# Differential attention in a two-layer decoder kernel: the first place with two steps of projection taken one unit earlier, and the norms of the second queries queued behind that place's weighing

## The chip, the cores and the metric

The kernel runs on one core of one Trainium2 chip. The metric is the device time of one execution in microseconds (us). The kernel before the change took 1323.74 us, the median of three runs (1322.02 to 1325.03).

## The reference, cut to what matters

The trunk has two layers over 512 tokens of width 1024. Layer 0 is a state-space mixer followed by a gated feed-forward block with a short causal convolution. Layer 1 is differential attention with 8 heads, followed by a second feed-forward block. The change lies in the attention of layer 1, whose core is this:

```python
q = (rms_norm(x, ln_g) @ q_w).reshape(b, s, ATT_HEADS, 2, ATT_HEAD_DIM)
q = rms_norm(q, q_norm_g)
...
logits = jnp.einsum('bqhcd,bkhcd->bhcqk', qblk, k).astype(jnp.float32) * scale
logits = logits + bias[None, :, None]
logits = jnp.where(dist >= 0, logits, -jnp.inf)
p = jax.nn.softmax(logits, axis=-1)
attn = p[:, :, 0] - lam * p[:, :, 1]
return jnp.einsum('bhqk,bkhd->bqhd', attn.astype(v.dtype), v)
...
o = rms_norm(o, subln_g) * (1.0 - lam_init)
return o.reshape(b, s, V_TOTAL) @ out_w
```

Each head has two softmax maps of 512 x 512, causal, which are subtracted with a learned weight. Keys and values come from the stream after layer 0, and they are computed once. Every query, and every head's output, is normed on its own.

## The kernel before, in words

Everything is float32. A large product is made of three TensorE matmuls over operands that are split into a high and a low part (`wh`, `wl` for a weight, `xgh`, `xgl` for the stream). Weights come in chunks: SyncE starts the load of a raw chunk (`wr_...`, three buffers), ScalarE writes its high half (`wh_...`, three buffers) and VectorE its low half (`wl_...`, three buffers).

The attention runs as one weave on TensorE, whose order is written out by hand. Two kinds of work are woven together.

**Units.** A head is cut into three units by rows of queries: part 0 holds the first two blocks of 128 queries, part 1 the third, part 2 the fourth. With 8 heads there are 24 units, counted by `t`; unit 10, for instance, is part 1 of head 3. A unit has four stages:

- `logits`: TensorE makes the logits of both maps (`lg`), VectorE adds the bias and finds the maximum (`mx`, line 1504), ScalarE takes the exponential (line 1512).
- `weigh`: VectorE subtracts the second map from the first (lines 1519 to 1525).
- `turn`: TensorE transposes the weighed map (`at`, line 1534), ScalarE copies it out of PSUM.
- `values`: TensorE multiplies by the values (`po`, line 1545), ScalarE scales the result into the head's output `ot` (line 1548).

When all three units of a head have their values, the head's output is normed: ScalarE squares it (`osq`, line 1555), VectorE sums it (`so`, line 1556), the reciprocal root is made in small steps on both engines (lines 494 to 499), and VectorE multiplies (`ot`, line 1558). Later `turned_out` transposes the normed output on TensorE (`oT`, line 1564); ScalarE and VectorE write its halves `oh` and `ol` (lines 1567 and 1568), which the output projection uses.

**Fill.** Between the stages of the units TensorE does steps of the projections that are still to come: the rest of the first half of the values, the second half of the queries (`q1`, heads 4 to 7), the second half of the values (`v1`), then the first part of the output projection. One `next(fill)` is one step: 12 matmuls of 512 columns, for two blocks of tokens (`ps_v1_0` and `ps_v1_1`, or `ps_v1_2` and `ps_v1_3`) and one chunk of weights (`wh_v1_0` is the chunk with rows 0 and 1 of the eight row blocks, `wh_v1_2` the next, and so on).

After the last step of `q1` its queries are normed (`head_norm`): VectorE multiplies four tiles `knq1_0` to `knq1_3` by the reciprocal root (line 1350). Their transposes (`ktq1_0` to `ktq1_3`, line 1357) are put in the list `late`; `proj` calls an entry of it when the step reaches the place that the entry names. Place (2, 0) is behind chunk 2, token block 0 of `v1`, and place (2, 1) behind token block 1. ScalarE copies the transposes to `qT1` (line 1358), which head 4 needs.

How many fill steps follow each unit is a list of numbers, `places`. At a place with one step and `t < 16`, the head output that is due (`out_of(t)`) is transposed ahead of the step. At a place with two steps it is transposed behind the first of them. A head's output is due five units after its last unit; head 1 is due at `t = 10`.

TensorE runs in the order of the program. On the other engines a scheduler picks the order when the program is built, and every engine then runs its own row of instructions in that fixed order. There are eight PSUM banks: four for the projections (`mm_bank`) and four for everything that is transposed or small (`aux_bank`), so that a new small tile waits until an earlier one has been read.

Of the kernel before, what the change touches and what calls it, by code (L numbers as in the profile page):

```python
# [13 lines left out]
ALU = mybir.AluOpType  # L14
# [4 lines left out]
P = 128  # L19
# [3 lines left out]
NT = T // P  # L23
# [18 lines left out]
def trunk_kernel(ctx: ExitStack, tc, x, ssm_ln_g, ssm_in_w, ssm_conv_w, ssm_conv_b, ssm_dt_bias,  # L42
# [4 lines left out]
    act, dve, pool, pe, sync = nc.scalar, nc.vector, nc.gpsimd, nc.tensor, nc.sync  # L47
# [14 lines left out]
    def aux_bank(name):  # L62
        return pp.tile([P, T], F32, tag="aux", name=name)
# [452 lines left out]
    def along_tokens(r, name):  # L516

        ps = aux_bank("al_" + name)
        for b in range(NT):
            pe.transpose(ps[:, b * P:(b + 1) * P], r[:, b:b + 1].to_broadcast([P, P]), ident)  # L520
        return ps
# [76 lines left out]
    with tc.tile_pool(name="ssm_y", bufs=1) as yp, tc.tile_pool(name="ssm", bufs=1) as sp:  # L598
# [29 lines left out]
        with tc.issue_after(b1_end.ins):  # L628
            for c in range(NT):
# [11 lines left out]
                          in1=dtb.unsqueeze(1).to_broadcast([P, NT, NH]), op=ALU.add)  # L641
# [7 lines left out]
        for n in (13, 11, 9, 7, 5, 3):  # L649
# [6 lines left out]
                                 in1=alog.unsqueeze(1).to_broadcast([P, NT, NH]),  # L656
# [228 lines left out]
        def normed(g, xs, rt):  # L885
            with tc.issue_after(state["last"]):
                r = along_tokens(rt, "g%d" % g)
            yh, yl = [], []
            for b in range(4):
                h = yp.tile([P, T], F32R, tag="yh", name="yh%d_%d" % (g, b), bufs=5)  # L890
                l = yp.tile([P, T], F32R, tag="yl", name="yl%d_%d" % (g, b), bufs=5)
                dve.scalar_tensor_tensor(out=xs[b], in0=xs[b], scalar=c2[:, 4 * g + b:4 * g + b + 1],
                                         in1=r, op0=ALU.mult, op1=ALU.mult)
                act.activation(h, xs[b], AF.Copy)
                dve.tensor_tensor(out=l, in0=xs[b], in1=h.bitcast(F32), op=ALU.subtract)
                yh.append(h)
                yl.append(l)
            return yh, yl
# [3 lines left out]
        for g in range(NG):  # L902
# [40 lines left out]
            else:  # L943
                op = out_proj(g - 1, *prev, None)
# [338 lines left out]
    with tc.tile_pool(name="att", bufs=1) as ap, ExitStack() as later:  # L1283
        rts = []
        late = []
# [59 lines left out]

        def head_norm(key, kn, ss, dst, gcol, where):
            rsqrt_act(ss, ap, key, [P, NT, 8], 64)
            for b in range(NT):
                v = kn[b].rearrange("p (a q) -> p a q", a=8)
                dve.tensor_tensor(out=v, in0=v, in1=ss[:, b, :].unsqueeze(2).to_broadcast([P, 8, 64]),  # L1350
                                  op=ALU.mult)

            def turned(bs):
                for b in bs:
                    ps = aux_bank("kt%s_%d" % (key, b))
                    for h in range(4):
                        pe.transpose(ps[:, h * P:(h + 1) * P], kn[b][:, h * P:(h + 1) * P], ident)
                    act.activation(dst[:, :, b * P:(b + 1) * P], ps.rearrange("p (h t) -> p h t", h=4),
                                   AF.Copy, scale=c2[:, gcol:gcol + 1])

            for at, bs in zip(where, ((0, 1), (2, 3))):
                late.append((at, lambda bs=bs: turned(bs)))
# [255 lines left out]
        with tc.manual_schedule(engines={mybir.EngineType.PE}):  # L1618
# [42 lines left out]
            def weigh_to(m):  # L1661
                nonlocal weighed
                while weighed < min(m, n):
                    us[weighed].weigh()
                    weighed += 1
# [4 lines left out]
                    values(valued)  # L1670
                    valued += 1

            for places in [(2, 2), 1, 1, 1, 1, 1, 1, 1, 1, 1, 2, 1, 1, 1, 1, 2, 1, 2, 1, 2, 1, 2, 2, 1, 1, 1]:
                if isinstance(places, tuple):
                    weigh_to(t)
                    turn_to(t - 1)
                    values_to(t - 2)
                    norm_heads()
                    turn_to(t)
                    next(fill)  # L1680
                    out_of(t + 1)
                    values_to(t)
                    norm_heads()
                    next(fill)
                    us[t].logits()
                    us[t + 1].logits()
                    weigh_to(t + 1)
                    next(fill)
                    weigh_to(t + 2)
                    next(fill)  # L1690
                    t += 2
                    continue
                turn_to(t - 1)
                if t == n - 5:
                    weigh_to(t)
                    with tc.issue_after(us[t - 1].weighed):
                        us[t].logits()
                elif t < n:
                    us[t].logits()
                weigh_to(t)  # L1700
                values_to(t - 2)
                for i in range(places):
                    if places == 1 and t < 16:
                        out_of(t)
                    next(fill)
                    if i == 0 and (places > 1 or t > n):
                        out_of(t)
                    if valued_heads and os:
                        with tc.issue_after(state["ol"]):
                            norm_heads()  # L1710
                    norm_heads()
                t += 1
# [40 lines left out]
```

## Time and profile before

| what | value |
|---|---|
| median of three runs | 1323.74 us |
| the profiled execution | 1323.59 us |
| its span in the trace | 1321.9 us |
| TensorE matmul busy | 1313.3 us, 99% of the span |
| VectorE busy | 1094.1 us, 83% |
| ScalarE busy | 722.5 us, 55% |
| GpSimd busy | 176.2 us, 13% |
| mean granted TensorE clock | 0.999 |

The profiled execution lies 0.15 us below the median of the runs, and 1.69 us of it lie outside the span. In the rows of the trace, PE is TensorE's matmul, PEld its load of weights, DVE is VectorE, ACT ScalarE, POOL GpSimd and SP SyncE. A row of the timeline gives the start in us from the span's start, the duration in us, engine, line, operation, what is written and what is read, how many instructions are merged, and in brackets the idle time ahead of it with the work that ended it. Matmuls overlap each other at their ends, so the step from one start to the next is what a matmul costs, not its duration.

### The profile page before, as it was taken

The numbers are of one execution on the slowest core, as the hardware profiler recorded it, in microseconds if no ns is written. First come the engines' busy times: TensorE is split into PE (matmuls) and PEld (weight loads), VectorE is DVE, ScalarE is ACT, GpSimd is POOL, SyncE is SP. The second block draws the span as 40 slices with busy tenths as digits, with TensorE's granted clock in tenths as the row PEclk, the third lists the DMA queues.
The fourth block names the chain that finished last, engine by engine and source line by source line (L and its number), as shares of the span: only waits on it lengthen the run. The fifth ranks groups of instructions, "written<-read, shape, count | busy, mean of one in ns | idle before, by whom it ended". The sixth has DMA issues, their size and how long they took to land. (4 is left out here: it accounts for less than half of the span.)

```text
span 1321.9 us, 18303 instructions
## 1 busy us (share of the span) xinstructions
PE 1313.3 (99%) x6771; PEld 1097.8 (83%) x6771; DVE 1094.1 (83%) x1834; ACT 722.5 (55%) x1176; POOL 176.2 (13%) x243
## 2 busy tenths in 40 slices
PE   9999999999999999999999999999999999999998
PEld 8878888888888988898889887767888878888887
DVE  7989888788878878886889877778778978887887
ACT  6696554743454545543556676767654534444452
POOL 4330200300121401110113210000020100010001
PEclk9999999999999999999999999999999999999999
DMA  7553533532235657674856854211225445453635
GB/s 209 161 154 87 146 108 103 145 92 79 80 96 149 118 149 205 167 155 128 225 143 143 208 129 125 64 57 56 65 80 159 97 119 178 106 99 112 191 64 128
DMA packets 202553, 167.85 MB, mean 127 GB/s; under 512 B 7580, under 2 KB 175904, under 8 KB 202464
## 3 DMA queue, kind: packets, MB, share of 16 engines
q1 hardware_dynamic: 176080, 124.93, 31.8%
q0 software_dynamic: 22928, 36.46, 14.8%
q10 hardware_dynamic: 3456, 5.30, 1.1%
q8 instruction: 53, 0.87, 0.3%
q14 instruction: 36, 0.29, 0.1%
HBM read 160.21 MB, written 6.44 MB: 126 GB/s over the span
## 5 line engine op out<-in xcount | busy, mean ns | idle before, releaser
L207 PE MATMUL ps_u<-xgh,wh_u 128*128 128x512 f32 x352 | 137.4, 390 | 0.0
L209 PE MATMUL ps_g<-xgh,wl_g 128*128 128x512 f32 x352 | 137.1, 389 | 0.0
L207 PE MATMUL ps_g<-xgh,wh_g 128*128 128x512 f32 x352 | 137.1, 389 | 0.0
L209 PE MATMUL ps_u<-xgh,wl_u 128*128 128x512 f32 x352 | 137.0, 389 | 0.0
L208 PE MATMUL ps_g<-xgl,wh_g 128*128 128x512 f32 x352 | 137.0, 389 | 0.0
L208 PE MATMUL ps_u<-xgl,wh_u 128*128 128x512 f32 x352 | 136.9, 389 | 0.0
L207 PE MATMUL ps_in<-xgh,wh_in 128*128 128x512 f32 x304 | 122.9, 404 | 0.0
L209 PE MATMUL ps_in<-xgh,wl_in 128*128 128x512 f32 x304 | 119.7, 394 | 0.0
L208 PE MATMUL ps_in<-xgl,wh_in 128*128 128x512 f32 x304 | 119.1, 392 | 0.0
L209 PEld LDWEIGHTS ps_g<-xgh,wl_g 128*128 128x128 f32 x352 | 66.1, 188 | 14.0 <-DVE wl_g L158 0.3
L208 PEld LDWEIGHTS ps_g<-xgl,wh_g 128*128 128x128 f32 x352 | 66.1, 188 | 13.7
L1228 PE MATMUL ps_s<-sl,wh_s 128*128 128x256 f32 x308 | 77.5, 283 | 0.0
L209 PEld LDWEIGHTS ps_u<-xgh,wl_u 128*128 128x128 f32 x352 | 66.1, 188 | 13.7
L1227 PE MATMUL ps_s<-sh,wh_s 128*128 128x256 f32 x308 | 77.5, 283 | 0.0
L208 PEld LDWEIGHTS ps_u<-xgl,wh_u 128*128 128x128 f32 x352 | 66.1, 188 | 13.6
L207 PEld LDWEIGHTS ps_g<-xgh,wh_g 128*128 128x128 f32 x352 | 66.1, 188 | 13.6
L207 PEld LDWEIGHTS ps_u<-xgh,wh_u 128*128 128x128 f32 x352 | 66.1, 188 | 13.5
L1118 ACT ACTIVATE sh<-vg 128x256 fp32r<-128x256 f32 (+1 forms) x44 | 23.0, 524 | 96.0 <-DVE vg L1266 96.0
L1047 POOL DMA_DIRECT2D wz<-in_ffn_down_w_dram x36 | 44.2, 1295 | 233.3 <-DVE wl_s L1075 156.1
L1262 ACT ACTIVATE vg<-vg 128x512 f32<-128x512 f32 x44 | 27.8, 633 | 78.7 <-DVE vg L1019 78.7
L1019 DVE SCALAR_TENSOR_TENSOR vg<-ug,cf,vg 128x511 f32<-128x511 f32 x88 | 65.8, 748 | 5.5 <-ACT vg L1017 4.1
L147 ACT ACTIVATE wh_u<-wr_u 128x1024 fp32r<-128x1024 f32 x44 | 46.6, 1059 | 42.5 <-PE ps_g L208 35.4
(430 smaller groups left out, 3527.1 us busy)
## 6 DMA issues: line engine op xcount, KB each, us to landing
wr_g<-in_ffn_up_w_dram SPq DMA_DIRECT2D x44, 512.0 KB, 3.9
wr_u<-in_ffn_up_w_dram SPq DMA_DIRECT2D x44, 512.0 KB, 4.0
wr_in<-in_ssm_in_w_dram SPq DMA_DIRECT2D x40, 512.0 KB, 3.9
wz<-in_ffn_down_w_dram POOLq DMA_DIRECT2D x27, 512.0 KB, 5.9
m<-cumd POOLq DMA_DIRECT2D x16, 512.0 KB, 5.0
wr_out<-in_ssm_out_w_dram SPq DMA_DIRECT2D x16, 512.0 KB, 3.5
wr_s<-in_ffn_down_w_dram SPq DMA_DIRECT2D x13, 512.0 KB, 3.8
xT<-in_ffn_down_w_dram SPq DMA_DIRECT2D x10, 512.0 KB, 7.0
```

Of the source, the lines that this page charges most:

```text
L147: return act.activation(self.wh[:, :self.n], self.raw[:, :self.n], AF.Copy)
L207: pe.matmul(ps, wh, xh, start=start, stop=False)
L208: pe.matmul(ps, wh, xl, start=False, stop=False)
L209: return pe.matmul(ps, wl, xh, start=False, stop=stop).ins
L1019: dve.scalar_tensor_tensor(out=v[:, s:], in0=u[:, :T - s], scalar=col(2 - s), in1=v[:, s:], op0=ALU.mult, op1=ALU.add)
L1047: pool.dma_start(view(t, nq), source(p0, c, nq, j, i), accum_op=ALU.add)
L1118: act.activation(sh[:, o], v, AF.Copy)
L1227: pe.matmul(v[:, b], wh[:, q, cols], h, start=q == 0, stop=False)
L1228: pe.matmul(v[:, b], wh[:, q, cols], w, start=False, stop=False)
L1262: act.activation(ga, ga, AF.Silu)
```

## The change

In `places`, the first single number 2 moves from unit 11 to unit 10. And the four multiplications that norm the second queries are no longer written where `head_norm` is called, but put in `late` with the place (0, 3): behind chunk 0, token block 3 of `v1`.

```diff
         def head_norm(key, kn, ss, dst, gcol, where):
             rsqrt_act(ss, ap, key, [P, NT, 8], 64)
-            for b in range(NT):
-                v = kn[b].rearrange("p (a q) -> p a q", a=8)
-                dve.tensor_tensor(out=v, in0=v, in1=ss[:, b, :].unsqueeze(2).to_broadcast([P, 8, 64]),
-                                  op=ALU.mult)
+            def normed():
+                for b in range(NT):
+                    v = kn[b].rearrange("p (a q) -> p a q", a=8)
+                    dve.tensor_tensor(out=v, in0=v, in1=ss[:, b, :].unsqueeze(2).to_broadcast([P, 8, 64]),
+                                      op=ALU.mult)
+
+            if key == "q1":
+                late.append(((0, 3), normed))
+            else:
+                normed()
...
-            for places in [(2, 2), 1, 1, 1, 1, 1, 1, 1, 1, 1, 2, 1, 1, 1, 1, 2, 1, 2, 1, 2, 1, 2, 2, 1, 1, 1]:
+            for places in [(2, 2), 1, 1, 1, 1, 1, 1, 1, 1, 2, 1, 1, 1, 1, 1, 2, 1, 2, 1, 2, 1, 2, 2, 1, 1, 1]:
```

The rows below give the order of instructions on an engine, cut to the places that the change moves. In the changed kernel all lines behind the edit stand six lower, so that L1570 there is L1564 before; L1350 becomes L1351. A number behind a tile's name counts buffers.

TensorE at units 10 and 11, before: `po2_1` are the values of part 1 of head 2, `oT1` the transposed output of head 1, `ps_v1_2` a fill step's first block, `at3_0`, `lg3_2` and `po2_2` the stages of unit 11's turn, `ktq1` the transposes of the second queries.

```order
L1545 MATMUL po2_1_8281<-vt2_6963,at2_1_8180 128x128
L1564 MATMUL oT1_8286<-ident_77,ot1_8028 128x128 x4
L1325 MATMUL ps_v1_2_8234<-wh_v1_0_7964,xgh_86 128x512
...
L1534 MATMUL at3_0_8308<-ident_77,lg3_0_0_8192 128x128 x3
L1498 MATMUL lg3_2_0_8317<-kT0_6957,qT0_6959 128x512
L1498 MATMUL lg3_2_1_8318<-kT0_6957,qT0_6959 128x512
L1545 MATMUL po2_2_8330<-vt0_6961,at2_2_8256 128x128
...
L1325 MATMUL ps_v1_0_8232<-wh_v1_2_8088,xgh_86 128x512
...
L1357 MATMUL ktq1_0_8350<-ident_77,knq1_0_8106 128x128 x4
L1357 MATMUL ktq1_1_8356<-ident_77,knq1_1_8111 128x128 x4
...
L1357 MATMUL ktq1_3_8374<-ident_77,knq1_3_8162 128x128 x4
```

The same place of TensorE with the change:

```order
L1551 MATMUL po2_1_8277<-vt2_6963,at2_1_8180 128x128
L1325 MATMUL ps_v1_2_8230<-wh_v1_0_7964,xgh_86 128x512
...
L1570 MATMUL oT1_8298<-ident_77,ot1_8028 128x128 x4
L1325 MATMUL ps_v1_0_8228<-wh_v1_2_8088,xgh_86 128x512
...
L1363 MATMUL ktq1_0_8321<-ident_77,knq1_0_8106 128x128 x4
L1363 MATMUL ktq1_1_8327<-ident_77,knq1_1_8111 128x128 x4
...
L1363 MATMUL ktq1_3_8345<-ident_77,knq1_3_8162 128x128 x4
L1540 MATMUL at3_0_8352<-ident_77,lg3_0_0_8192 128x128 x3
L1504 MATMUL lg3_2_0_8361<-kT0_6957,qT0_6959 128x512
L1504 MATMUL lg3_2_1_8362<-kT0_6957,qT0_6959 128x512
L1551 MATMUL po2_2_8374<-vt0_6961,at2_2_8252 128x128
```

The 12 matmuls of the step with `ps_v1_2` and `ps_v1_3` now stand ahead of `oT1`, and the next step, with the transposes of the queries, stands ahead of unit 11's `at3_0`, `lg3_2` and `po2_2`. The number of instructions on TensorE is the same.

VectorE from the normed output of head 1 to the low half of its transpose, before: `lg3_0_0` is the weighing of unit 9 in its two pieces, `knq1` the norms of the second queries, `ol1` the low half of `oT1`.

```order
L1558 TENSOR_TENSOR ot1_8028<-ot1_8028,so1_8168 128x512
...
L1525 SCALAR_TENSOR_TENSOR lg3_0_0_8192<-lg3_0_1_8193,sm3_0_8191,lg3_0_0_8192 128x128
L1350 TENSOR_TENSOR knq1_0_8106<-knq1_0_8106,ssq1_7751 128x512
...
L1350 TENSOR_TENSOR knq1_3_8162<-knq1_3_8162,ssq1_7751 128x512
L1525 SCALAR_TENSOR_TENSOR lg3_0_0_8192<-lg3_0_1_8193,sm3_0_8191,lg3_0_0_8192 128x256
L1568 SCALAR_TENSOR_TENSOR ol1_8292<-oT1_8286,c2_89,oh1_8291 128x512
```

The same place of VectorE with the change; `wl_v1_6` is the low half of a chunk of weights:

```order
L1564 TENSOR_TENSOR ot1_8028<-ot1_8028,so1_8168 128x512
...
L1531 SCALAR_TENSOR_TENSOR lg3_0_0_8192<-lg3_0_1_8193,sm3_0_8191,lg3_0_0_8192 128x128
L1531 SCALAR_TENSOR_TENSOR lg3_0_0_8192<-lg3_0_1_8193,sm3_0_8191,lg3_0_0_8192 128x256
L1351 TENSOR_TENSOR knq1_0_8106<-knq1_0_8106,ssq1_7751 128x512
...
L1351 TENSOR_TENSOR knq1_3_8162<-knq1_3_8162,ssq1_7751 128x512
L1574 SCALAR_TENSOR_TENSOR ol1_8304<-oT1_8298,c2_89,oh1_8303 128x512
L173 SCALAR_TENSOR_TENSOR wl_v1_6_8310<-wr_v1_6_8307,c2_89,wh_v1_6_8309 128x512 x2
```

The second piece of unit 9's weighing goes from behind the four norms to ahead of them. Everything on VectorE up to the normed output of head 1 keeps its order.

ScalarE behind the last exponential of unit 10, before: `oh1` is the high half of `oT1`, `wh_v1_6` the high half of a chunk, in two pieces, `at3_0` the copy of unit 9's transposed map.

```order
L1512 ACTIVATE lg3_1_1_8266,sm3_1_8264<-lg3_1_1_8266,mx3_1_8263 128x384
L1567 ACTIVATE oh1_8291<-oT1_8286,c2_89 128x512
L172 ACTIVATE wh_v1_6_8338<-wr_v1_6_8336,c2_89 128x512
L1535 ACTIVATE at3_0_8307<-at3_0_8308 128x384
L172 ACTIVATE wh_v1_6_8338<-wr_v1_6_8336,c2_89 128x512
```

The same place of ScalarE with the change; `qT1` are the copies of the transposed queries:

```order
L1518 ACTIVATE lg3_1_1_8262,sm3_1_8260<-lg3_1_1_8262,mx3_1_8259 128x384
L172 ACTIVATE wh_v1_6_8309<-wr_v1_6_8307,c2_89 128x512
L1573 ACTIVATE oh1_8303<-oT1_8298,c2_89 128x512
L172 ACTIVATE wh_v1_6_8309<-wr_v1_6_8307,c2_89 128x512
L1364 ACTIVATE qT1_6960<-ktq1_0_8321,c2_89 128x4x128
...
L1364 ACTIVATE qT1_6960<-ktq1_3_8345,c2_89 128x4x128
L1541 ACTIVATE at3_0_8351<-at3_0_8352 128x384
```

The first piece of `wh_v1_6` now stands ahead of `oh1`, and the four copies of the transposed queries stand ahead of the copy of unit 9's map. SyncE's and GpSimd's rows, all transfers among them, keep their order.

## The prediction

> **What bounds the kernel now.** I read the page's busy times first, then the waits of TensorE, then the timeline round the place of the change.
>
> ```profile
> span 1321.9 us, 18303 instructions
> PE 1313.3 (99%) x6771; PEld 1097.8 (83%) x6771; DVE 1094.1 (83%) x1834; ACT 722.5 (55%) x1176; POOL 176.2 (13%) x243
> PE oT L1564 <- DVE ot L1558: 2.8, 1, 2.8
> ```
>
> TensorE is busy for 1313.3 us of a span of 1321.9 us, so time can only go where TensorE does less, or idles less, or runs at a better clock. The change leaves its matmuls as many as they were. Of the waits that the view names, the largest is a single one of 2.8 us: the transpose of a head's normed output (`oT`) for VectorE's multiplication. The timeline shows it at unit 10, the very place that the change reorders:
>
> ```profile
> 861.91 0.94 PE L1545 MATMUL po<-vt,at 128*128 128x128 f32 x6
> 865.61 1.03 PE L1564 MATMUL oT<-ident,ot 128*128 128x128 f32 x4 [2.76 <-DVE ot L1558]
> 866.30 0.78 PE L1325 MATMUL ps_v<-wh_v,xgh 128*128 128x512 f32 x1
> ...
> 868.58 0.63 PE L1327 MATMUL ps_v<-wh_v,xgl 128*128 128x512 f32 x1
> 869.00 0.47 PE L1325 MATMUL ps_v<-wh_v,xgh 128*128 128x512 f32 x1
> ```
>
> The wait costs more than itself. The windows view (length; busy time and count of PE, PEld, DVE, ACT, POOL; granted clock; transfers) has the whole piece from `po2_1` to the next projection step, the same kinds and counts of work at units 13 and 14, where nothing waits, and then the idle stretch and the one behind it:
>
> ```profile
> 861.91:872.86 10.95, 8.19 (x40) 6.19 (x38) 8.43 (x30) 6.68 (x22) 0.00 (x0) 0.84 0.17 49
> 886.41:892.79 6.38, 6.38 (x39) 4.88 (x38) 4.66 (x13) 3.72 (x9) 0.00 (x0) 1.00 0.01 3
> 862.85:865.61 2.76, 0.00 (x0) 0.00 (x1) 2.15 (x13) 2.65 (x11) 0.00 (x0) 1.00 0.65 190
> 865.61:869.00 3.39, 3.39 (x10) 2.82 (x11) 3.39 (x10) 1.38 (x5) 0.00 (x0) 0.52 0.01 2
> ```
>
> 10.95 us against 6.38: this piece loses 4.57 us. 2.76 are idle; and for 3.39 us behind it the granted clock is 0.52, so that matmuls stand 0.42 us apart (868.58 to 869.00) where they stand 0.23 apart elsewhere. That second part is worth about 1.57: the four transposes and six matmuls took 3.39, and by the rows below they take 0.35 + 1.47.
>
> [...]
>
> **The change, part by part.** It adds and removes no instruction. It moves 12 matmuls (`ps_v1_2`, `ps_v1_3`) ahead of `oT1`, and the next step of 12, with the 16 transposes of the second queries, ahead of unit 11's `at3_0`, `lg3_2` and `po2_2`. These rows carry the steps between starts:
>
> ```profile
> 857.01 0.94 PE L1545 MATMUL po<-vt,at 128*128 128x128 f32 x6
> 857.70 0.47 PE L1325 MATMUL ps_v<-wh_v,xgh 128*128 128x512 f32 x1
> 860.54 0.60 PE L1534 MATMUL at<-ident,lg 128*128 128x128 f32 x4
> ...
> 872.86 0.48 PE L1325 MATMUL ps_v<-wh_v,xgh 128*128 128x512 f32 x1
> 874.33 1.04 PE L1357 MATMUL ktq<-ident,knq 128*128 128x128 f32 x8
> 875.12 0.47 PE L1325 MATMUL ps_v<-wh_v,xgh 128*128 128x512 f32 x1
> 876.58 1.04 PE L1357 MATMUL ktq<-ident,knq 128*128 128x128 f32 x8
> 877.38 0.47 PE L1325 MATMUL ps_v<-wh_v,xgh 128*128 128x512 f32 x1
> ...
> 887.19 0.60 PE L1564 MATMUL oT<-ident,ot 128*128 128x128 f32 x4
> 887.54 0.47 PE L1325 MATMUL ps_v<-wh_v,xgh 128*128 128x512 f32 x1
> 890.40 0.49 PE L1534 MATMUL at<-ident,lg 128*128 128x128 f32 x3
> ...
> 892.79 0.48 PE L1325 MATMUL ps_v<-wh_v,xgh 128*128 128x512 f32 x1
> ```
>
> A `po` costs 0.69, twelve matmuls 2.84, an `oT` 0.35, six matmuls 1.47, eight query transposes 0.79, then 1.46 and 0.80, and the piece `at`, `lg`, `po` of units like 11 costs 2.39.
>
> *`oT1`.* Up to the normed output `ot1` VectorE's order is unchanged, and nothing that it needs is moved on TensorE. So `po2_1` starts at 861.91 as now, the twelve matmuls at 862.60, and `oT1` is reached at 862.60 + 2.84 = 865.44. VectorE's rows:
>
> ```profile
> 861.73 0.75 DVE L173 SCALAR_TENSOR_TENSOR wl_v<-wr_v,c,wh_v 128x512 fp32r<-128x512 f32 x1
> ...
> 864.87 0.68 DVE L1558 TENSOR_TENSOR ot<-ot,so 128x512 f32<-128x512 f32 x1
> ...
> 865.83 0.35 DVE L1525 SCALAR_TENSOR_TENSOR lg<-lg,sm,lg 128x128 f32<-128x128 f32 x1
> 866.10 2.49 DVE L1350 TENSOR_TENSOR knq<-knq,ssq 128x512 f32<-128x512 f32 x4
> 868.50 0.48 DVE L1525 SCALAR_TENSOR_TENSOR lg<-lg,sm,lg 128x256 f32<-128x256 f32 x1
> 868.90 0.74 DVE L1568 SCALAR_TENSOR_TENSOR ol<-oT,c,oh 128x512 fp32r<-128x512 f32 x1
> ```
>
> `ot1` ends at 865.55, and `oT1` then started at 865.61, 0.06 behind it. The wait shrinks from 2.76 to about 0.17, which lies under the end of the matmul ahead (0.39 long, started at 865.21). So the 12 matmuls cover it; if that cover were gone, the price would be the 4.57 again. The next step starts at 865.61 + 0.35 = 865.96; its weights are done, since VectorE writes the last low half of the chunk after it at 861.73.
>
> *The norms.* The second piece of unit 9's weighing costs 0.40 from start to start (868.50 to 868.90) and now stands ahead. The norms go from 866.10 to 866.50, one every 0.60 (2.40 for four), so `knq1_0` is ready at 866.50 + 0.69 = 867.19 and `knq1_1` at 867.79. TensorE gets there at 865.96 + 1.47 = 867.43 and half of 0.79 later, 867.83. With 0.06 for the signal that is 0.18 of room for the first and none for the second: a price of 0 to 0.1, of which I take 0. The move costs nothing while the six matmuls cover it, and up to 0.4 without them. It is unit 9's weighing that profits, and `at3_0` isn't due before 870.
>
> *The banks.* In the built order the fourth query transpose waits for `ol1`, which must have read the PSUM bank of `oT1`. `ol1` is now queued behind the norms on VectorE, as it was, and `oh1` behind the first piece of `wh_v1_6` on ScalarE, as it was not:
>
> ```profile
> 866.12 0.19 ACT L1512 ACTIVATION_READ_ACCUMULATOR lg<-lg,mx 128x1 f32 x1
> 866.68 0.69 ACT L1567 ACTIVATE oh<-oT,c 128x512 fp32r<-128x512 f32 x1 [0.38 <-PE oT L1564]
> 870.66 0.72 ACT L172 ACTIVATE wh_v<-wr_v,c 128x512 fp32r<-128x512 f32 x1 [3.29 <-PE ps_v L1327]
> 875.60 1.24 ACT L1358 ACTIVATE qT<-ktq,c 128x512 f32<-128x512 f32 x2
> L139 SPq DMA_DIRECT2D wr_v<-in_kv_w_dram x8: 367/368/373, 758.0 to 838.1; - x8
> DMA to landing us min/median/max: 3.6/4.0/5.0
> ```
>
> That piece of `wh_v1_6` waited until 870.66 for the last matmul on its old buffer (`wh_v1_0`). With the change that matmul ends at 865.67, so ScalarE starts it at 866.31, when it is free; `oh1` follows at 867.0 and ends at 867.7; VectorE, free at 868.90, does `ol1` until 869.64. The fourth query transpose is due half of 0.80 behind 865.96 + 1.47 + 0.79 + 1.46 = 869.68, at 870.08: 0.4 of room. The last load of `wr_v` was issued at 838.1 and took 5.0 at most, so its data are 23 us early. The four copies to `qT1`, 0.62 each, then end at about 871.6; unit 11's `po2_2`, which takes the last of their banks, is due at 871.95. Price 0, bounded by 0 and 0.3.
>
> *Sum.* The transposes end at 869.68 + 0.80 = 870.48, `at3_0` to `po2_2` take 2.39, and the step with `ps_v1_2` of the next chunk starts at 872.87. Before it started at 877.38. That is 4.51 us earlier. What follows keeps its distances: the loads, splits and norms there wait for work that moves along, and VectorE's and ScalarE's order changes only until unit 13. The gain lies between 4.57 (no new wait) and 4.57 - 0.17 - 0.1 - 0.3 = 4.0; I take 4.5. Against the profiled execution, 1323.59 - 4.5 = 1319.1; that execution stands 0.15 below the median of the runs, so I predict **1319.2 us**. With the runs' own scatter (1322.02 to 1325.03, so 1.7 down and 1.3 up) the likeliest case covers 1317.5 to 1321.0.
>
> **The rivals.** About 0.2%, 2.65 us, is what a measurement of this kernel can tell from no change: the line lies at 1321.1.
>
> *A, the wait goes and the slow clock stays.* If the stretch at 0.52 has another cause than the idle time, only 4.5 - 1.57 = 2.9 is gained: 1320.8. For it speaks that a shorter idle time did nothing to the clock (0.72 us idle ahead of this stretch in the last feed-forward block):
>
> ```profile
> 1065.48 1.21 PE L1133 MATMUL ps_s<-wl_s,sh 128*128 128x512 f32 x4 [0.72 <-DVE wl_s L1075]
> 1065.48:1068.87 3.39, 3.39 (x14) 2.58 (x15) 3.39 (x5) 2.12 (x2) 0.00 (x0) 1.00 0.00 0
> ```
>
> Against it speaks that the slow stretch begins in the instant in which the idle time ends. 6%. [...]
>
> *B, a shorter wait moves to the query transposes.* They come 6.9 us earlier on TensorE (874.33 to 867.43), the norms 0.4 later. Each microsecond by which VectorE is late costs TensorE one. Two norms late, 1.2, gives 1320.4; with the slow clock on top, 1.57, 1322.0. Against it stands only the 0.18 and 0.0 of room worked out above, so it isn't far away: 10%.
>
> *C, it is given back.* Between `ol1` and unit 12's logits VectorE idles 1.70 and 3.04, and the change presses that stretch together by 4.5. If VectorE couldn't use those gaps, units 12 and 13 would wait for their maxima, and up to all of it is lost: 1322 to 1323.7. Against it: both gaps are waits for ScalarE's pieces of weights, which wait for TensorE and so move along. 6%.
>
> ```profile
> 871.42 0.75 DVE L173 SCALAR_TENSOR_TENSOR wl_v<-wr_v,c,wh_v 128x512 fp32r<-128x512 f32 x1 [1.70 <-ACT wh_v L172]
> 881.52 1.22 DVE L158 TENSOR_TENSOR wl_ao<-wr_ao,wh_ao 128x1024 fp32r<-128x1024 f32 x1 [3.04 <-ACT wh_ao L147]
> ```
>
> *D, slower: `oh1` behind `wh_v1_6`.* If ScalarE's piece of weights isn't released early, `oh1`, `ol1`, the fourth query transpose and the four copies queue behind it. Were it to start at 870.66 as before, `oh1` would end at 872.0, `ol1` at 872.7, and TensorE would idle 2.7, pay 1.57 for the clock and about 1 for the copies: 5.3 against the 4.5, 1324.5. From a start at 872.5 on it is over 1326.4. Nothing in the rows delays it, 5%.
>
> *That the change doesn't do what it says* is excluded by the order of the rows.
>
> **How the numbers follow.** Forecast 73%, A 6%, B 10%, C 6%, D 5%. The forecast lies 1.9 below the line, a little more than the runs' scatter; I give 5 of its 73 to "same". A and B are split by the line: 5 and 5 of them are faster, 1 and 5 the same. C is the same; D is half slower, half same, and 2 more go to "slower" for what I haven't seen, taken from the forecast. Faster 0.76, same 0.19, slower 0.05. The range 1317.3 to 1322.3 holds the forecast, A and B, and leaves out most of C and D.
>
> **What will show it.** Right: no `oT` waiting for `ot` among TensorE's waits; the first piece of `ps_v1_2` 0.7 behind `po2_1`; the clock at 1.00 from 857 to 880; the next chunk's `ps_v1_2` at about 872.9; TensorE's busy time lower by the 1.6 of the slow stretch while the span falls by 4.5. Wrong: a new wait of `ktq` for `knq` (B) or for `ol` (D), a clock below 1 with no idle time ahead (A), or idle time of `lg` and `at` at units 12 to 14 (C).

## The result, and the profile after

The changed kernel took 1319.99 us, the median of 9 runs (1319.46 to 1320.79), against 1323.74 us for the kernel before on the same chip (9 runs, 1322.02 to 1325.03; the same median and range were given for three at the start). The ratio is 0.9973, with a 95% interval of 0.9965 to 0.9982: 0.27% faster. The profiled execution took 1319.46 us against 1323.59, 4.13 less. The forecast was 1319.2 us.

The page's busy times of the changed kernel, and in a second fence the two longest of TensorE's waits (us in total, times, longest):

```profile
span 1317.8 us, 18303 instructions
PE 1311.9 (100%) x6771; PEld 1096.5 (83%) x6771; DVE 1093.6 (83%) x1834; ACT 722.3 (55%) x1176; POOL 179.0 (14%) x243
```

```profile
PE warm L291 <- DVE ones L218: 1.1, 1, 1.1
PE ps_s L1133 <- DVE wl_s L1075: 0.7, 1, 0.7
```

The wait of `oT` for `ot`, 2.8 us before, is no longer among them. TensorE is busy for 1.4 us less, with as many matmuls as before, and the span is 4.1 us shorter. The timeline of TensorE in the changed kernel, at the place that the prediction works through:

```profile
862.08 0.94 PE L1551 MATMUL po<-vt,at 128*128 128x128 f32 x6
862.77 0.48 PE L1325 MATMUL ps_v<-wh_v,xgh 128*128 128x512 f32 x1
...
865.78 0.66 PE L1570 MATMUL oT<-ident,ot 128*128 128x128 f32 x4
866.20 0.48 PE L1325 MATMUL ps_v<-wh_v,xgh 128*128 128x512 f32 x1
...
867.68 1.03 PE L1363 MATMUL ktq<-ident,knq 128*128 128x128 f32 x8
...
869.95 1.03 PE L1363 MATMUL ktq<-ident,knq 128*128 128x128 f32 x8
870.82 0.49 PE L1540 MATMUL at<-ident,lg 128*128 128x128 f32 x3
871.25 1.21 PE L1504 MATMUL lg<-kT,qT 64*128 64x512 f32 x4
872.38 1.16 PE L1551 MATMUL po<-vt,at 128*128 128x128 f32 x8
873.29 0.48 PE L1325 MATMUL ps_v<-wh_v,xgh 128*128 128x512 f32 x1
```

Nothing in these rows stands idle for a named reason. From `po2_1` to the next chunk's `ps_v1_2` it is 873.29 - 862.08 = 11.21 us, where it was 877.38 - 861.91 = 15.47: 4.26 less. I call this stretch **the piece** from here on; it holds the same matmuls in every kernel below (two, told there, add 11 and 7). The windows of the changed kernel (length; busy time and count of PE, PEld, DVE, ACT, POOL; granted clock; transfers):

```profile
861.91:872.86 10.95, 10.94 (x63) 8.36 (x62) 9.78 (x32) 9.04 (x26) 0.00 (x0) 1.00 0.18 58
857.00:900.00 43.00, 42.99 (x243) 32.73 (x240) 34.01 (x118) 33.99 (x91) 0.00 (x0) 1.00 0.21 67
```

The first row is the window that before held 8.19 us of TensorE's work at a clock of 0.84. It is full now, at 1.00, and it stays so to 900.

The timeline of VectorE at the same place of the changed kernel, and of ScalarE in the last row:

```profile
865.04 0.69 DVE L1564 TENSOR_TENSOR ot<-ot,so 128x512 f32<-128x512 f32 x1
...
866.00 0.75 DVE L1531 SCALAR_TENSOR_TENSOR lg<-lg,sm,lg 128x128 f32<-128x128 f32 x2
866.66 2.49 DVE L1351 TENSOR_TENSOR knq<-knq,ssq 128x512 f32<-128x512 f32 x4
869.07 0.75 DVE L1574 SCALAR_TENSOR_TENSOR ol<-oT,c,oh 128x512 fp32r<-128x512 f32 x1
...
867.00 0.66 ACT L1573 ACTIVATE oh<-oT,c 128x512 fp32r<-128x512 f32 x1
```

`ot1` is no earlier than it was (it ends at 865.73, before at 865.55, and the whole trace is shifted by 0.17 from its first microseconds). It is TensorE that comes later.

### The profile page after: what moved, and what is told of

Its sections match the earlier page's. It is cut to its first block, busy times and chain, and to the rows that moved or that the text cites. A ratio compares the mean times of both kernels' runs of the same rounds, so it can differ in the third digit from the quotient of the medians.

```text
span 1317.8 us, 18303 instructions
## 1 busy us (share of the span) xinstructions
PE 1311.9 (100%) x6771; PEld 1096.5 (83%) x6771; DVE 1093.6 (83%) x1834; ACT 722.3 (55%) x1176; POOL 179.0 (14%) x243
```

## The experiments

Twelve runs were made, each against the kernel before on the same chip: e1 to e4 on one chip, e5 to e8, e9 to e11 and e12 on three others. Rows of different chips are best compared by their ratios. The table cuts each profiled span in three: from its start to `po2_1`, the piece, and from there to the end. The first row is the kernel before, the second the changed one.

| run | start to `po2_1` | piece | rest of the span | TensorE waits in the piece | median, us | ratio to before, 95% interval |
|---|---|---|---|---|---|---|
| before | 861.91 | 15.47 | 444.5 | `oT` 2.76 | 1323.74 | |
| change | 862.08 | 11.21 | 444.5 | none named | 1319.99 | 0.9973 [0.9965, 0.9982] |
| e1, places only | 862.51 | 11.20 | 444.5 | none named | 1319.46 | 0.9965 [0.9952, 0.9977] |
| e2, late transposes | 862.19 | 15.58 | 444.4 | `at` 2.41 | 1324.24 | 1.0001 [0.9992, 1.001] |
| e3, 11 extra matmuls | 861.65 | 15.02 | 444.3 | bank 1.31 | 1323.43 | 0.9996 [0.9988, 1.0005] |
| e4, change again | 862.60 | 11.22 | 444.8 | none named | 1319.97 | 0.9969 [0.9956, 0.9981] |
| e5, late transposes and norms | 862.83 | 11.57 | 444.5 | none named | 1320.19 | 0.9969 [0.9958, 0.9981] |
| e6, norms only | 861.63 | 15.34 | 444.4 | `oT` 2.77 | 1323.86 | 0.9996 [0.9987, 1.0005] |
| e7, own squares | 862.22 | 13.56 | 444.5 | bank 1.06, `at` 0.89 | 1322.05 | 0.9985 [0.9976, 0.9995] |
| e8, norms, own squares | 862.65 | 12.15 | 444.4 | bank 1.06 | 1320.40 | 0.9972 [0.9961, 0.9984] |
| e9, 7 extra matmuls | 861.95 | 14.05 | 444.4 | bank 1.29 | 1322.67 | 0.9992 [0.9983, 1.0001] |
| e10, change, slow norms | 862.97 | 11.74 | 444.5 | `oT` 0.55 | 1320.37 | 0.9973 [0.9963, 0.9982] |
| e11, change, own squares | 861.70 | 10.96 | 444.4 | none named | 1319.63 | 0.9967 [0.9955, 0.9980] |
| e12, change, late first norm | 862.75 | 12.26 | 444.4 | `ktq` 0.86 | 1320.18 | 0.9975 [0.9966, 0.9985] |

Three readings of the table itself. The rest of the span is 444.3 to 444.8 us whatever the piece was: what the piece gains is kept to the end. The start, in which no edit moves anything on TensorE, scatters by 1.3 us (861.63 to 862.97). It scatters with one and the same kernel too: the traces of the change and of e4 differ by 0.52 there, and between 5 and 7 us TensorE did 15 matmuls in the one and 11 in the other. And the medians follow the piece: the median less the piece lies between 1307.92 (e12) and 1308.78 us (change) in all fourteen rows.

### Which of the two edits does it: e1, e6 and e4

e1 is the change without the edit of the norms:

```diff
-            for places in [(2, 2), 1, 1, 1, 1, 1, 1, 1, 1, 1, 2, 1, 1, 1, 1, 2, 1, 2, 1, 2, 1, 2, 2, 1, 1, 1]:
+            for places in [(2, 2), 1, 1, 1, 1, 1, 1, 1, 1, 2, 1, 1, 1, 1, 1, 2, 1, 2, 1, 2, 1, 2, 2, 1, 1, 1]:
```

> Only the list of places is changed; the four norms of the second queries stay where they were written, so on VectorE they stay ahead of the second piece of unit 9's weighing. Theory (the whole gain is oT1's wait and the slow clock behind it, and the norms only fill in): the wait is gone here too, knq1_0 is even ready 0.4 us earlier, and the time equals that of the full change, 1319.6 to 1320.4 us, a ratio to before of 0.997. Rival (the norms are what gives TensorE room): a wait of the query transposes shows, and the time is 1 to 3 us above the full change.

The theory held. Its piece is 11.20 us against 11.22 of the change on the same chip (e4, the changed kernel again), and no query transposes wait. Its median, 1319.46, lies 0.14 below the expected range; the runs of e1 (1318.85 to 1319.90) and of e4 (1318.98 to 1320.33) overlap.

> The full change once more, on the same chip and against the same runs of before as the other three, so that they can be compared with it. Theory: a gain of 3.6 to 4.3 us, 1319.5 to 1320.2 us, and a trace whose piece from po2_1 to the next chunk's ps_v1_2 is again about 4.26 us shorter than before. Rival (the gain depends on the chip or on the phase of the clock's window): a gain below 3 us or above 5.

The change came out as the first time: 4.10 us less than before, and a piece shorter by 4.25. What the traces show of a window of the clock, which the rival speaks of, are steps of 3.41 us (last section); the piece was 11.21 us in the change's trace and 11.22 in e4's.

e6 is the edit of the norms without the places:

```diff
...
+            if key == "q1":
+                late.append(((0, 3), normed))
+            else:
+                normed()
```

> Only the second edit of the change: the norms of the second queries behind the weighing, with the list of places as before. Theory: TensorE still stands for oT1, whose operand isn't touched by the norms; the wait stays at 2.4 to 2.8 us with the slow clock behind it, 1323.3 to 1324.5 us (ratio 0.9995 to 1.0005). Rival (the norms' place is what holds the weighing, and so a part of the loss): 1320 to 1322.5.

Its waits of TensorE still show the old one:

```profile
PE oT L1570 <- DVE ot L1564: 2.8, 1, 2.8
```

The theory held: 1323.86 us, ratio 0.9996, no difference that can be measured. So the gain belongs to the list of places, all of it. Beside the moved places, the edit of the norms gives nothing, and alone it gives nothing either. It isn't idle in every order, though, as e2 and e5 show.

### Is it only the wait for ot1: e2 and e5

If all of the loss hung on `ot1`, it should be enough to let TensorE do the one step that follows unit 10 ahead of `oT1`, with the list of places unchanged:

```diff
-                    if places == 1 and t < 16:
+                    if places == 1 and t < 16 and t != 10:
...
-                    if i == 0 and (places > 1 or t > n):
+                    if i == 0 and (places > 1 or t > n or t == 10):
```

> Smallest edit that takes the wait away: the places stay as before, but at unit 10 the transpose of head 1's output stands behind its one step of projection instead of ahead of it; nothing else is moved on TensorE. Theory: oT1 finds its operand ready within 0.2 us, the clock stays at 1.00, and the time falls by as much as with the full change, to 1319.5 to 1320.5 us. Rival (moving the second step and the query transposes forward is worth something by itself): less than two thirds of the full change's gain, above 1321.2 us.

The theory missed. The wait of `oT` was gone, and the time was that of before: 1324.24 us. The timeline of e2, of TensorE and, behind the dots, of VectorE:

```profile
865.91 0.66 PE L1564 MATMUL oT<-ident,ot 128*128 128x128 f32 x4
866.62 0.30 PE L1534 MATMUL at<-ident,lg 128*128 128x128 f32 x1
869.33 0.51 PE L1534 MATMUL at<-ident,lg 128*128 128x128 f32 x2 [2.41 <-DVE lg L1525]
...
866.39 2.49 DVE L1350 TENSOR_TENSOR knq<-knq,ssq 128x512 f32<-128x512 f32 x4
868.80 0.48 DVE L1525 SCALAR_TENSOR_TENSOR lg<-lg,sm,lg 128x256 f32<-128x256 f32 x1
```

TensorE stood again, one tile further on: `at3_0` wants the second piece of unit 9's weighing, and VectorE does the four norms first. Two operands are late in this place, one behind the other, and `oT1`'s wait had hidden the second. The windows of e2 show the idle stretch and the 3.39 us behind it:

```profile
866.92:869.33 2.41, 0.00 (x0) 0.00 (x0) 2.41 (x6) 1.48 (x3) 0.00 (x0) 1.00 0.00 0
869.33:872.72 3.39, 3.39 (x10) 1.64 (x11) 2.16 (x7) 0.49 (x1) 0.00 (x0) 0.53 0.00 0
```

e5 adds the edit of the norms to e2, which puts the weighing ahead of them; the places stay as before.

> The list of places stays as before (two steps of projection at unit 11, one at unit 10). At unit 10 the transposes of ot1 are put behind the one step instead of ahead of it, as in the second experiment, and the norms of the second queries go in line behind the weighing of unit 9's second piece, as the change puts them. Theory (two operands are late in this place: ot1 for its transposes, and behind it the weighing that at3_0 transposes; the first late operand needs one step of projection, the second needs either the second step or the norms out of its way): oT1 has its step of 0.7 us and more behind po2_1, the weighing ends near 866.6 and at3_0 is due at about the same time; no wait over 1 us, no slow clock, 11.2 to 11.6 us from po2_1 to the next chunk's ps_v1_2 where before took 15.47, and 1319.5 to 1320.5 us (ratio 0.9965 to 0.9975). Rival (only the second step at unit 10 covers it, whatever VectorE's order): at3_0 or oT1 waits 2 us or more, the clock falls, and the time is 1322 to 1324.5.

The theory held: 1320.19 us and no named wait of TensorE in the piece. The timeline of e5, of TensorE and, behind the dots, of VectorE, where the weighing stands ahead of the norms:

```profile
866.52 0.66 PE L1570 MATMUL oT<-ident,ot 128*128 128x128 f32 x4
867.24 0.74 PE L1540 MATMUL at<-ident,lg 128*128 128x128 f32 x3
...
866.74 0.75 DVE L1531 SCALAR_TENSOR_TENSOR lg<-lg,sm,lg 128x128 f32<-128x128 f32 x2
867.40 2.49 DVE L1351 TENSOR_TENSOR knq<-knq,ssq 128x512 f32<-128x512 f32 x4
```

So there are two ways to the same end. Two steps of projection at unit 10 put `at3_0` so late that the weighing may stand behind the norms (e1); with one step there, the norms have to give way (e5). e5's piece is 0.36 us longer than the change's, since the weighing is still just late: its second piece ends at 867.49, when `at3_0` has already begun. From `oT1` to `lg3_2` (867.91) e5 takes 1.39 us, where the change's steps behind `oT1` and behind `at3_0` take 0.42 + 0.43; some of this comes back at other steps.

### Why ot1 is late, and a third thing that is late: e7, e8 and e11

The squares of head 1's output and those of the second queries share one buffer, and before, the former waited for a sum over the latter. e7 is the kernel before with a buffer of its own for head 1's squares:

```diff
-            sq = ap.tile([P, T], F32, tag="ksq", name="osq%d" % h, bufs=1)
...
-            act.activation(sq, fl(ot), AF.Square)
-            dve.reduce_sum(so, sq.rearrange("p (a q) -> p a q", a=NT), axis=AX.X)
+            if h == 1:
+                for i in range(2):
+                    sq = up.tile([P, 256], F32, tag="osq1", name="osq1_%d" % i, bufs=1)
+                    act.activation(sq, fl(ot)[:, 256 * i:256 * (i + 1)], AF.Square)
+                    dve.reduce_sum(so[:, 2 * i:2 * i + 2], sq.rearrange("p (a q) -> p a q", a=2), axis=AX.X)
+            else:
+                ...
```

> Neither edit of the change. The squares of head 1's output get a buffer of their own (in two halves of 256 columns: two activations and two reductions in place of one each), so that they need not wait until the squares of the second queries, which use the same buffer, are summed. Theory (two late operands): ot1 is ready about 1 us or more earlier and oT1's wait goes or falls under 1 us, but VectorE then does the four norms ahead of unit 9's weighing, and at3_0 waits 2 to 3 us for that with the slow clock behind: 1322.5 to 1324.5 us (ratio 0.999 to 1.0005). Rival (the shared buffer is the whole cause of the lost 4.5 us): no wait over 1 us, 1319.3 to 1320.5.

1322.05 us, outside both expectations. The waits of TensorE in e7, and then `ot1` and the norms in VectorE's timeline:

```profile
PE oT L1570 <- DVE mx L1504: 1.1, 1, 1.1
PE at L1534 <- DVE lg L1525: 0.9, 1, 0.9
```

```profile
860.98 0.68 DVE L1564 TENSOR_TENSOR ot<-ot,so 128x512 f32<-128x512 f32 x1
...
864.67 2.49 DVE L1350 TENSOR_TENSOR knq<-knq,ssq 128x512 f32<-128x512 f32 x4
```

`ot1` is done at 861.66, ahead of `po2_1` at 862.22, so the shared buffer is why it was late. And `oT1` still waits 1.06 us, for a maximum of VectorE (`mx`), which reads unit 10's logits: it is the PSUM bank that is late now, since a small tile takes a bank only when an earlier one has been read. `at3_0` waits for the weighing as the theory said, but 0.89 us and not 2 to 3, since the norms began earlier too, 2.45 us behind `po2_1` (before: 866.10 - 861.91 = 4.19). So both operands came earlier, and both waits are left, in a shorter form that brings no slow clock (1.00 over the 3.39 us behind each).

e8 is e7 with the edit of the norms:

> The buffer of their own for the squares of head 1's output, as in the seventh, and the norms of the second queries behind the weighing; the list of places as before. Theory (two late operands, each now early by its own means, without any step moved): neither oT1 nor at3_0 waits more than 1 us, the clock stays at 1.00 between 862 and 872, and the time is 1319.5 to 1321 us (ratio 0.9965 to 0.998). Rival (the place needs TensorE work that does not depend on VectorE, and order alone doesn't give it): a wait of 2 us or more and 1322.5 to 1324.5.

`at3_0`'s wait is gone, that for the bank stays at 1.06 (a little over the 1 us that the theory allowed), and 1320.40 us lies where the theory put it. By the table, e7 to e8, taking the weighing out from behind the norms is worth 1.41 us of the piece in this order.

e11 is the change with a buffer of its own for the squares:

> The changed kernel with a buffer of their own for the squares of head 1's output (two halves, as in the seventh experiment), so that ot1 is ready about 3.5 us earlier and oT1 follows its step at once. Theory (nothing but a remainder of some 0.2 us is left in this place): piece 11.0 to 11.2 us, 1319.4 to 1320.1 us (ratio 0.9962 to 0.9972 to the kernel before, the same as the change within what the runs can tell). Rival (the two extra small instructions push the norms, and the query transposes wait): piece 11.4 to 12 us, 1320.2 to 1321.

The theory held, with a piece slightly below its range: 10.96 us, 0.25 less than the change, and 1319.63 us. Against the change (1319.97 in e4) and e1 (1319.46) no difference can be told, so this is no better version that a measurement could show. It shows what is left in the place: `oT1` follows its step 0.16 sooner (865.24 - 862.39 = 2.85 us behind the step's start, where the change has 3.01), and it costs 0.35 and not 0.42.

### The slow clock: e3 and e9

In e3 and e9 the kernel before gets matmuls with nothing to wait for into the gap, in the bank of `oT1`, whose transposes then overwrite them; 11 in e3 and 7 in e9:

```diff
+            if h == 1:
+                for _ in range(7):
+                    pe.matmul(ps, xgh[0][:, :P], xgh[0], start=True, stop=True)
```

> The kernel before with eleven extra matmuls of 512 columns (0.23 us each, 2.5 us in all) into the bank of oT1 just ahead of oT1, whose results are overwritten: TensorE works through the wait, and nothing else is moved. Theory (the slow clock comes from the idle time): oT1 still starts at about 865.6 us, the granted clock behind it stays at 1.00, and the kernel gains the 1.57 us that the slow stretch cost, 1322.0 to 1322.4 us. Rival A (the slow stretch has another cause): the clock behind oT1 is about 0.52 as before and the time stays at 1323.7 us.

> The kernel before, with 7 extra matmuls of 512 columns put into the bank of oT1 ahead of its transposes (their result is overwritten), where the third experiment had 11: those 11 ran 863.9 to 866.6 and so pushed oT1 itself about 1 us back. With 7 they end near 865.6, when ot1 is there. Theory (the slow clock comes from the one long idle of 2.76 us, and two idles of 1.3 and 0.7 us do not bring it): the wait for ot1 stays as long as before in sum, the clock stays at 1.00, the piece from po2_1 to the next chunk's ps_v1_2 is 13.8 to 14.2 us (15.47 less the 1.57 of the clock), and the time is 1322.2 to 1322.9 us (ratio 0.9985 to 0.999). Rival (idle time counts in sum over a window, however it is cut): the clock falls behind oT1 all the same, piece 15.2 to 15.6 us, 1323.6 to 1324.3.

They couldn't start at once, but had to wait for the bank, as in e7. The 11 of e3 then ran longer than `ot1` was late, so that `oT1` came 4.92 us behind its `po2_1`, against 3.95 in e9. In e3 the clock stayed at 1.00, as its theory had it, but with `oT1` later by more than 1 us its time, 1323.43 us, lies in neither expected range and says little. In e9 the theory held: the extra matmuls end about when `ot1` is there (865.58). Its timeline, and in a second fence the windows of the idle stretch and of the 3.39 us behind it:

```profile
864.18 1.89 PE L1565 MATMUL oT<-xgh 128*128 128x512 f32 x7 [1.29 <-DVE mx L1504]
865.90 0.60 PE L1567 MATMUL oT<-ident,ot 128*128 128x128 f32 x4
```

```profile
862.89:864.18 1.29, 0.00 (x0) 0.00 (x1) 0.69 (x5) 1.29 (x7) 0.00 (x0) 1.00 0.38 82
864.18:867.57 3.39, 3.39 (x17) 2.82 (x18) 3.39 (x15) 2.74 (x8) 0.00 (x0) 1.00 0.36 124
```

`oT1` starts 3.95 us behind `po2_1` (before: 3.70), so the wait for `ot1` is paid in full. What is saved is the slow clock alone: the piece is 15.47 - 14.05 = 1.42 us shorter. The median is 1.19 less, but its interval just reaches 1, so it is the trace that shows this. The 3.39 us that ran at 0.52 before run at 1.00. The slow clock is a price of the long idle stretch (2.76 us, with 0.52 behind it; 1.29 us here, with 1.00), and it goes with it.

### How much room VectorE has: e10 and e12

e10 puts two operations on VectorE ahead of the norms in the changed kernel:

```diff
+                for _ in range(2 if key == "q1" else 0):
+                    dve.scalar_tensor_tensor(out=kn[0], in0=kn[0], scalar=1.0, in1=kn[0], op0=ALU.mult, op1=ALU.max)
```

> The changed kernel, with two operations on VectorE ahead of the norms of the second queries (each takes the larger of the first tile and itself, so the values stay; about 0.75 us each, 1.35 in line). Theory (VectorE is just in time for the query transposes behind the change: the prediction reckoned a room of 0.18 us): the first query transposes wait 1.0 to 1.2 us, the second pair is covered by that, the clock stays at 1.00, and about 1.0 to 1.2 us of the gain are lost: 1320.9 to 1321.4 us, piece 12.2 to 12.5 us. Rival (VectorE has slack in this place, as its later gap of 1.26 us would suggest): no wait over 0.4 us and 1319.9 to 1320.4.

It didn't ask what it was meant to. The scheduler put the two operations where their operand was ready, at 853.8 and 856.2, more than 10 us ahead of the norms (867.8). There they made `ot1` later: `oT` waits 0.55 us, the piece is 11.74, and 1320.37 us is in the range of the rival, which this can't support. The only thing to read from it is that these two operations, 0.68 us each and ahead of `ot1`, cost 11.74 - 11.21 = 0.53 of the piece.

e12 makes the operation depend on the first norm, so that it can stand nowhere else:

```diff
+                    for _ in range(1 if key == "q1" and b == 0 else 0):
+                        dve.scalar_tensor_tensor(out=kn[0], in0=kn[0], scalar=1.0, in1=kn[0], op0=ALU.mult, op1=ALU.max)
```

> The changed kernel with one more operation on VectorE on the first normed tile of the second queries (the larger of the tile and itself, so its values stay). It needs the first norm and so can't stand elsewhere: in the built order it is third, behind the norms of the first and the second tile. By the changed kernel's rows the first norm started at 866.66 and a norm costs 0.60, so the tile is final at 866.66 + 0.60 + 0.60 + 0.75 = 868.61, where TensorE took it at 867.68. Theory (the prediction's rival B: each microsecond by which VectorE is late here costs TensorE one): the query transposes wait 0.9 to 1.1 us, nothing behind them waits, the clock stays at 1.00, the piece is 12.1 to 12.4 us and the time 1320.7 to 1321.3 us. Rival (TensorE's later waits or VectorE's gaps give it back): a piece of 11.2 to 11.6 us and 1319.8 to 1320.4.

The timeline of e12, of TensorE and, behind the dots, of VectorE:

```profile
869.37 1.06 PE L1365 MATMUL ktq<-ident,knq 128*128 128x128 f32 x8 [0.86 <-DVE knq L1354]
...
868.54 0.69 DVE L1354 SCALAR_TENSOR_TENSOR knq<-knq 128x512 f32<-128x512 f32 x1
```

In the trace the theory holds: the query transposes wait 0.86 us, nothing behind them waits, and the piece is 12.26, 1.05 longer than that of the change. The profiled execution pays it to its end, with a rest of 444.4 us. The median, 1320.18, fits the rival instead: only 0.2 us above e4's. Its ten runs fall into two groups, six from 1319.89 to 1320.26 and four, the profiled one among them, from 1321.01 to 1321.14, no further apart than the start scatters in the table. The price of the wait is shown by the rows; that every run pays it is not shown by these medians.

## Why the prediction was right, point by point

**The place and the direction** were right. The wait of `oT1` went, and TensorE's piece became shorter by it and by the slow clock.

**`oT1`.** Reckoned: start 3.70 us behind `po2_1`, where 3.53 would be without a wait. Measured: 865.78 - 862.08 = 3.70. e11, with `ot1` early, has 3.54.

**The norms.** The price of 0 was right (e1 against e4). The sentence that "`at3_0` isn't due before 870" turned out to carry more than it was given. It was written as the reason why unit 9's weighing profits; in truth the gain rests on it. Had only `oT1` been covered, as in e2, `at3_0` would have been due at 866.6, the norms would have stood in its way, and nothing would have been gained. The prediction compared the piece with units 13 and 14, where neither operand is late, and so had the whole loss of 4.57 right; it put all of it on `ot1`, and that was wrong. The bank, which holds `oT1` up for 1.06 us when `ot1` is early (e7), isn't in the prediction either. The moved steps together cover all three; for the bank, which the prediction hadn't reckoned with, that is luck.

**The slow clock.** The prediction let it begin in the instant in which the idle time ends. It is near that here, but not tied to it: at 0.50 the clock stands from 865.74 to 869.15, 0.13 us behind the end of the idle time, and in e6 it begins 0.25 us ahead of that end (last section). That the idle time brings it held (e9). Its price was reckoned at 1.57; from `oT1` on, e9 is 1.67 shorter than before (876.00 - 865.90 = 10.10 against 877.38 - 865.61 = 11.77). TensorE's busy time fell by 1.4, where 1.6 was forecast.

**The banks behind it.** `ol1` was reckoned at 868.90 and started at 869.07, which is the shift of 0.17; `oh1`, reckoned at 867.0, started at 867.00, so 0.17 earlier than reckoned; and there was no wait of the query transposes or of `po2_2`. Price 0 held.

**The sum** is the step that was a little off: 4.5 reckoned, 4.26 measured in the piece, within the bounds of 4.0 and 4.57. The missing 0.25 are terms that were taken from other neighbours: `oT` cost 866.20 - 865.78 = 0.42 and not 0.35; `at` behind query transposes followed after 870.82 - 869.95 = 0.87, where 0.80 was taken from a matmul behind them; `lg3_2` cost 872.38 - 871.25 = 1.13 and not 1.06; and some hundredths in the steps. e11 gets the first of them back, and 0.16 ahead of it. The other two are in every kernel with the new places (0.88 and 1.14 in e11). Why `lg3_2` costs 0.07 more there no run tells.

**From the piece to the time.** The start of the profiled execution took 0.17 longer, so 4.26 became 4.1 in the span and 4.13 in its time. The medians differ by 3.75 in the first comparison and by 4.10 in the second (e4). The first is less than 4.13 because the changed kernel's profiled execution is the fastest of its nine runs, 0.53 below their median, while that of before lies 0.15 below its own. So the forecast of 1319.2 was 0.79 too low: for the profiled execution it meant 1319.1, which is 0.36 too low, and the rest is where the two executions lie among their runs. With a start that scatters by 1.3 us the runs don't tell 3.75 or 4.10 from 4.26.

**The rivals.** *A* (the slow clock has another cause) is refuted by e9, where it goes while `oT1` still comes as late. *B* did not occur, but its price is right: in e12 the query transposes start 2.91 us behind `oT1` (869.37 - 866.46) and not 1.90, so 1.01 later, and the piece lost 1.05. *C* (given back later) is refuted by the rest of the span, 444.5 us in both kernels. *D* (`oh1` behind `wh_v1_6`) did not occur; no run was made to bring it about, so its price stays an argument.

## What to carry to other kernels

When an engine that sets the time waits for one late operand, look for the next operand in its row that is late too: the first wait hides it, and a cure for the first alone may move the wait and gain nothing (e2: 2.41 us at `at` for 2.76 at `oT`, 1324.24 us). Work that depends on nothing late covers all of them at once when it is taken from behind the last of them and put ahead (e1: no named wait, 1319.46 us); taken from between them, it only moves the wait (e2). To hurry the operand uncovers them one by one (e7: waits of 1.06 and 0.89 us). And a step's price belongs to its neighbours (`oT` cost 0.42 us in the change and 0.35 in the row from which it was reckoned): take it from a row where the same two kinds of work follow each other.

## What the runs showed of the hardware that was not expected

**Idle time and the clock.** In these traces idle stretches of 2.76, 2.77 (e6) and 2.41 us (e2) on TensorE were each followed by a granted clock of 0.52 to 0.53 over the 3.39 us behind them. Behind idle stretches of 1.31 (e3), 1.29 (e9), 1.06 and 0.89 (e7), and 0.86 us (e12) it stood at 1.00.

Cut where the granted clock changes, the windows of before (first two rows) and of e6 (last two) show more:

```profile
862.33:865.74 3.41, 0.65 (x6) 0.46 (x5) 2.60 (x17) 3.30 (x16) 0.00 (x0) 1.00 0.53 154
865.74:869.15 3.41, 3.41 (x11) 2.83 (x12) 3.41 (x9) 1.25 (x3) 0.00 (x0) 0.50 0.01 2
861.67:865.08 3.41, 0.89 (x8) 0.70 (x6) 2.60 (x14) 3.30 (x15) 0.00 (x0) 1.00 0.46 153
865.08:868.49 3.41, 3.16 (x10) 2.68 (x11) 3.10 (x10) 1.63 (x5) 0.00 (x0) 0.50 0.01 3
```

The slow stretch is 3.41 us at 0.50, and it need not begin where the idle time ends: before, that is at 865.61, in e6 at 865.33. In all fourteen traces the granted clock changes only at whole steps of 3.41 us, counted from its first record in the trace (before: 865.74 - 5.58 = 860.16 us at 1.00, 252 steps, and then the one at 0.50). Cut into such steps, the traces agree. Where TensorE was busy for 1.33 us of a step or less, the next step ran at 0.50: 0.65 before, 0.89 in e6, 0.94 in e2, and 0.75 to 1.33 in the last whole step of nine traces (0.97 in the change, 1.33 in e11). Where it was busy for 1.55 or more, the next ran at 1.00: 2.10 in e3, 2.12 in e9, 2.36 in e7, and 1.55 to 2.60 in the last whole step of the other five (1.86 before, 1.55 in e9). So it is the idle time within one step that counts here, and the line lies between 1.33 and 1.55 us of work in 3.41. Whether one gap or several take up a step, no run tells. The count begins between 3.98 (e3) and 7.25 us (e12) behind the start of the span.

**The price differs from run to run.** Of 64 runs of the kernel before that stood beside e1 to e11, 5 had a mean clock of 1.000 and took 1322.06 to 1323.06 us, 36 had 0.999 with a median of 1323.80, 18 had 0.998 with 1324.26, and 5 had 0.997 with 1324.88. Of 36 runs of the kernels without a long wait (e1, e4, e5, e8, e10 and e11) none had less than 0.999. One slow step takes 3.41 x 0.50 / 1322 = 0.0013 off the mean of a run of 1322 us, so the five runs of 1.000 can't hold it: they didn't pay. A mean of 0.997 takes nearly two such steps (an estimate from the same sum), and no trace shows where the second lies. The groups between say less, because a slow step at the very end, where TensorE has nothing left to do, counts in the mean too (in the trace of the change 1316.47 to 1317.77, at 0.50, with no matmul in it). A gap of 2.76 us that lies across the border of two steps can leave more than 1.55 us of work in each. That would explain the runs that don't pay, but no trace of such a run was kept, so this stays an argument.
